# One pool of 2 KB pieces for the second mixer and the expert layer, seven weight chunks made of pieces, and a gather in fp32 from the residual stream

## The chip, the cores and the metric

The kernel runs on one core of a Trainium2 chip. The metric is the device time of one execution in microseconds (us), taken as the median of several runs. Lower is better. The engines are TensorE (PE in the rows, its weight loads PEld), VectorE (DVE), ScalarE (ACT), GpSimd (POOL) and SyncE (SP), which here only issues transfers; 16 DMA engines move data between DRAM and the on-chip memory of 128 partitions.

## What is computed

Two layers of an encoder over 256 tokens of width 1024. Each layer has a token mixer (attention, RWKV-7, pooling and convolution in four groups of columns) and a channel mixer: a dense SwiGLU in the first layer, and eight experts of which each token takes two in the second. The change touches the memory of the second mixer and the whole of the expert layer, which computes this (the reference sorts the tokens by expert; the sum is the same):

```python
h = rms_norm(x, norm_g[l, 2]) * (1.0 + sc_f) + sh_f
logits = xf @ router_w                       # 256 x 8
top_val, top_idx = lax.top_k(logits, 2)
gates = jax.nn.softmax(top_val, axis=-1)
# for every expert e, over the tokens that chose it:
y_e = (jax.nn.silu(xblk @ w1[e]) * (xblk @ w3[e])) @ w2[e]
out = out.at[tok].add(y_e * gate[:, None])
x = x + gt_f * rms_norm(out, norm_g[l, 3])
```

An expert's three matrices are 1024 x 3584, 1024 x 3584 and 3584 x 1024 in fp32, so the eight experts are 336 MB of weights, and every one of them is read once for a few dozen tokens.

## The kernel before

The program is laid out by a recording layer and pools: the code says what reads and writes which tile, a tile pool decides when its memory may be taken again, and the order in which an engine's instructions stand is made from that. The stages follow one another: modulation, mixer 0, dense layer, mixer 1, expert layer. In the profiled execution the last one begins at about 640 us.

**Weights of the experts.** The packed weights of an expert are 42 chunks (`NCH`) of 128 partitions x 2048 fp32, 1 MB each: 28 for the first two matrices and 14 for the third. `weights()` (L970) hands out the next buffer of a ring of 13 and issues its load on SyncE, with no condition but that the buffer's last reader is done. The ring has three kinds: three `raw` buffers and four pairs `hi`, `lo` of half the width, which earlier stages use for their own weights, and six (`MRAW`) of the expert layer's own, `mw`. A `raw` or `mw` chunk is one DMA, with 8 KB per partition in a row (L985); a pair is two DMAs with 4 KB rows (L979). A DMA on SyncE also waits until the one eight places ahead of it has landed, and SyncE issues in one fixed order, so whatever waits there holds back all that stands behind.

**One expert.** `up()` takes the chunks of the first two matrices (products `u`), `gated()` makes silu(u1) x u3 and transposes it (`sg`, `sT`), `down()` takes the chunks of the third (`y`). This goes in four pieces of the hidden width (`SUP`, index `s`), with `down` of one piece behind `up` of the next. The tokens of an expert sit in up to 96 places (`CAP`), in three groups of 32; the third is computed only if there are more than 64 tokens. `outputs()` and `back()` then spread the result over the 256 tokens (`yhl`, `oT`), weight it and add it to `yac`.

**Router and gather.** The router's logits `lg` come from matmuls `pl`; VectorE picks the two best (`MAX`, `MAX_INDEX`), makes `selb`, and TensorE the places of the tokens (`pos`), from which `posm`. The gather is a matmul with a one-hot matrix `oh`. Since a product in the format fp32r (a faster format of less precision) is inexact, the normalised tokens are first split into a high part `hh` and a low part `hl` by `natural()` (L1038 to L1042), and `gather()` (L1056) runs two fp32r matmuls for each block, for two experts at once (2 x 96 columns). It is called by `prepare()` for a pair of experts: at the start, and for the next pair in piece `s == 1` of every second expert.

**The place where the layer starts.** `count()` counts the tokens of each expert (`cnt`), and decides whether any has more than 96 (`of`). `over(0)` reads that flag into a register on several engines, SyncE among them, with a TENSOR_LOAD (L1305), to run a further round if needed; for this input none runs. The load stands in SyncE's order among the DMAs of the weights, where the recording put it. TensorE and others read their own counts.

**Memory.** The mixers use 36 `slots` of [128, 512] fp32 (`NSLOT`) and 38 of [128, 256] (`NHALF`) in a pool of their own that closes at the mixer's end; the expert layer has separate tiles.

## Time and profile before

| what | us |
|---|---|
| median of 3 runs (lowest to highest) | 1511.33 (1510.83 to 1512.97) |
| the profiled execution's own time | 1509.55 |
| its span, first to last instruction | 1507.8 |
| TensorE busy | 1400.7 |
| VectorE busy | 609.9 |
| ScalarE busy | 391.9 |
| GpSimd busy | 1.8 |

The share of TensorE is 93% of the span, and its mean granted clock 0.992 of full speed. The times of the three runs lie within 0.15% of each other. The rows that follow below come from the one profiled execution; microseconds in them count from the start of its span. The page shows the span in 40 equal slices (37.7 us each), with the rate of the transfers in GB/s in each. A table of stretches gives, for every stretch, the busy time of each engine with the number of its instructions, then the granted clock, the share of time in which the 16 DMA engines are busy, and the rate. A timeline lists instructions in order of time, those of one kind in a row together: start, time from the first start to the last end, engine, line, operation, output <- inputs, shapes, count, and in brackets how long the engine idled before and what it waited for. For SyncE it shows the issue of DMAs, not their transfer.

### The profile page before, as it was taken

What the parts mean: (1) busy time and instruction counts of PE and PEld (TensorE: products, weight loads), DVE (VectorE), ACT (ScalarE), POOL (GpSimd) and SP (SyncE); (2) the same over time, 40 slices, a digit from 0 to 9 for tenths busy, and PEclk for the clock granted to TensorE, in tenths of its full rate; (3) what the DMA queues carried; (4) which work ended last, traced back from release to release, by engine and by line L of the source; (5) the groups of instructions that cost most, each with busy time, mean ns of one, the idle gap of its engine ahead of it and who ended that gap; (6) DMA issues with size and microseconds to landing.
All of it is one profiled execution on the core that took longest, in us unless ns stands there. A gap on an engine that the chain in (4) does not pass through costs nothing. (4 is left out here: it accounts for less than half of the span.)

```text
span 1507.8 us, 30915 instructions
## 1 busy us (share of the span) xinstructions
PE 1400.7 (93%) x13541; PEld 824.0 (55%) x13566; DVE 609.9 (40%) x1202; ACT 391.9 (26%) x744; POOL 1.8 (0%) x19
## 2 busy tenths in 40 slices
PE   3999989999998999989898999999999999998885
PEld 2997779999997987733232333333433334332222
DVE  7698879888836785531020020020020200210203
ACT  4744464444438643420020000010000010000101
POOL 0000000000000000000000000000000000000000
PEclk9999999999999999999999999999999999999998
DMA  9554659978733421579999999999999999999994
GB/s 375 207 202 136 205 231 388 367 290 313 291 137 130 158 79 37 216 300 417 418 416 416 416 415 416 416 411 379 416 416 415 416 417 416 416 404 412 416 409 198
DMA packets 85262, 487.43 MB, mean 323 GB/s; under 512 B 9841, under 2 KB 10225, under 8 KB 40946
## 3 DMA queue, kind: packets, MB, share of 16 engines
q1 hardware_dynamic: 83522, 482.45, 80.3%
q10 hardware_dynamic: 1584, 2.68, 0.6%
q8 instruction: 124, 2.03, 0.5%
q14 instruction: 32, 0.26, 0.0%
HBM read 484.05 MB, written 1.05 MB: 322 GB/s over the span
## 5 line engine op out<-in xcount | busy, mean ns | idle before, releaser
L167 PE MATMUL u<-mw,xe 128*32 128x512 f32 (+1 forms) x3368 | 358.6, 537 | 22.2 <-DMA mw<-in_moe_dram 18.0
L1158 DVE TENSOR_TENSOR sg<-sg,u 128x256 f32<-128x256 f32 (+1 forms) x96 | 34.3, 381 | 651.3 <-ACT sg L1157 651.3
L167 PEld LDWEIGHTS u<-mw,xe 128*32 128x32 f32 x3368 | 115.1, 109 | 218.2 <-issue 159.8
L1157 ACT ACTIVATE sg<-u 128x256 f32<-128x256 f32 (+1 forms) x96 | 30.8, 356 | 666.8 <-PE u L167 657.4
L167 PE MATMUL y<-mw,sT 128*32 128x512 f32 x1480 | 180.9, 594 | 18.7 <-DMA mw<-in_moe_dram 13.4
L218 DVE TENSOR_TENSOR wlo<-raw,whi 128x1024 fp32r<-128x1024 f32 x142 | 170.2, 1222 | 51.9 <-ACT whi L217 51.5
L217 ACT ACTIVATE whi<-raw 128x1024 fp32r<-128x1024 f32 x142 | 147.1, 1057 | 146.5 <-issue 50.4
L167 PE MATMUL u<-mwhi,xe 128*32 128x512 f32 (+1 forms) x748 | 172.2, 551 | 1.8 <-DMA mwhi<-in_moe_dram 1.0
L167 PE MATMUL u<-mwlo,xe 128*32 128x512 f32 (+1 forms) x748 | 151.4, 551 | 1.5 <-issue 0.8
L171 PE MATMUL g<-hlo,whi 128*128 128x256 f32 x448 | 127.1, 284 | 0.2
L170 PE MATMUL g<-hhi,whi 128*128 128x256 f32 x448 | 127.1, 284 | 0.0
L172 PE MATMUL g<-hhi,wlo 128*128 128x256 f32 x448 | 126.8, 283 | 0.0
L167 PEld LDWEIGHTS y<-mw,sT 128*32 128x32 f32 x1480 | 53.2, 109 | 129.8 <-issue 84.0
L254 DVE CUSTOM_DVE_ANT_0 raw<-raw,row,pcs 128x1024 f32<-128x1024 f32 x96 | 120.3, 1279 | 4.2 <-ACT row L1341 3.7
L167 PE MATMUL y<-mwhi,sT 128*32 128x512 f32 x324 | 95.8, 594 | 0.0
L170 PE MATMUL z<-hhi,whi 128*128 128x256 f32 x304 | 88.1, 290 | 3.8 <-ACT whi L217 3.7
L167 PEld LDWEIGHTS u<-mwhi,xe 128*32 128x32 f32 x748 | 46.9, 109 | 79.1 <-issue 69.1
L172 PE MATMUL z<-hhi,wlo 128*128 128x256 f32 x304 | 87.2, 287 | 2.4 <-DVE wlo L218 2.4
L171 PE MATMUL z<-hlo,whi 128*128 128x256 f32 x304 | 88.1, 290 | 0.2
L171 PEld LDWEIGHTS g<-hlo,whi 128*128 128x128 f32 x448 | 86.1, 192 | 1.2 <-DVE hlo L336 0.7
L170 PEld LDWEIGHTS g<-hhi,whi 128*128 128x128 f32 x448 | 86.2, 193 | 0.6
L172 PEld LDWEIGHTS g<-hhi,wlo 128*128 128x128 f32 x448 | 86.2, 192 | 0.0
(302 smaller groups left out, 1825.0 us busy)
## 6 DMA issues: line engine op xcount, KB each, us to landing
mw<-in_moe_dram SPq DMA_DIRECT2D x232, 1024.0 KB, 15.1
mwlo<-in_moe_dram SPq DMA_DIRECT2D x104, 512.0 KB, 12.6
mwhi<-in_moe_dram SPq DMA_DIRECT2D x104, 512.0 KB, 13.8
raw<-in_ada_dram SPq DMA_DIRECT2D x44, 1024.0 KB, 6.6
raw<-in_ffn_dram SPq DMA_DIRECT2D x42, 1024.0 KB, 7.0
raw<-in_win_dram SPq DMA_DIRECT2D x20, 1024.0 KB, 4.8
raw<-in_wout_dram SPq DMA_DIRECT2D x6, 1024.0 KB, 4.9
raw<-in_ada_dram SPq DMA_DIRECT2D x8, 512.0 KB, 6.9
```

What stands on the lines that cost most here:

```text
L167: pe.matmul(o, a, b, start=start, stop=stop)
L170: pe.matmul(o, ah, bh, start=start, stop=False)
L171: pe.matmul(o, ah, bl, start=False, stop=False)
L172: pe.matmul(o, al, bh, start=False, stop=stop)
L217: ops[0].append(act.activation(hi, raw[:, c], AF.Copy))
L218: ops[1].append(dve.tensor_sub(lo, raw[:, c], hi.bitcast(F32)))
L254: r = dve.tensor_tensor_reduce(w, w, cB, scale=1.0, scalar=P(l, "ab", v * KB + k), op0=OP.mult, op1=OP.add, accum_out=mods[l][:, v, k:k + 1])
L1157: other_set(act.activation(sg, u[:, 0:w], AF.Silu))
L1158: dve.tensor_mul(sg, sg, u[:, w:2 * w])
```

## The change

- One pool for mixer 1 and the expert layer: 55 slots of [128, 512] fp32, 2 KB per partition. It stays open from mixer 1 to the end; mixer 0 has a pool of the same form that closes. The 38 half-size tiles of the mixers are now halves of slots (`halves`), made in pairs.
- The ring of weight buffers has 17 chunks, in this order: seven of kind `slots`, each of four slots and loaded with four DMAs with 2 KB rows; three `raw`; four pairs; three `mw` (`MRAW` from 6 to 3).
- The expert layer's other large tiles (`hT`, `yac`, `oh`, `xe`, `dg`, `oT`, `sg`, `sT`, `yhl`) are slots too, and `prow` lies in the memory of an earlier constant.
- `natural()`, `hh` and `hl` go. The gather is an fp32 matmul from the residual stream `xr` with `oh` scaled by the norm `rs`, one expert at a time (96 columns), prepared in piece `s == 1` of every expert but the last.
- The loads `lr`, `c` and `pw` of mixer 1, which stood behind three loads of its weights, now stand among the loads of the dense layer.

```diff
-NSLOT = 36
-NHALF = 38
-MRAW = 6
+NSLOT = 55
+MRAW = 3
+MSLOT = 7
...
+    def slots(st, name):
+
+        sp = st.enter_context(tc.tile_pool(name=name, bufs=1, reuse_waits="tile"))
+        return lambda name, dt=F32: sp.tile([128, 512], dt, name=name, tag="s", bufs=NSLOT)
...
-            def half(name):
-                return mp.tile([128, 256], F32, name=name, tag="h", bufs=NHALF).rearrange("p (n f) -> p n f", n=4)
+            def halves(name):
+                t = slot_(name).rearrange("p (e n f) -> p e n f", e=2, n=4)
+                return [t[:, e] for e in range(2)]
...
-            ring = ["raw"] * NR + ["half"] * (2 * NH) + ["m"] * MRAW
+            ring = ["slots"] * MSLOT + ["raw"] * NR + ["half"] * (2 * NH) + ["m"] * MRAW
             mw = {"n": 0}
 
             def weights(src, first=None):
                 kind = ring[mw["n"] % len(ring)]
                 mw["n"] += 1
-                if kind == "half":
-                    hs = [wp.tile([128, 1024], F32, name="mw" + t, tag=t, bufs=2 * NH) for t in ("hi", "lo")]
-                    for i, h in enumerate(hs):
-                        nc.sync.dma_start(h, src[:, i * 1024:(i + 1) * 1024])
-                    return lambda c, n: hs[c // 1024][:, c % 1024:c % 1024 + n]
-                if kind == "raw":
-                    t = wp.tile([128, 2048], F32, name="mw", tag="raw", bufs=NR)
+                if kind == "slots":
+                    ts = [slot_("mws") for _ in range(4)]
+                elif kind == "half":
+                    ts = [wp.tile([128, 1024], F32, name="mw" + t, tag=t, bufs=2 * NH) for t in ("hi", "lo")]
+                elif kind == "raw":
+                    ts = [wp.tile([128, 2048], F32, name="mw", tag="raw", bufs=NR)]
                 else:
-                    t = ep.tile([128, 2048], F32, name="mw", tag="mw", bufs=MRAW)
-                nc.sync.dma_start(t, src)
-                return lambda c, n: t[:, c:c + n]
-
-            hh = one.tile([128, 2, D], F32R, name="hh")
-            hl = one.tile([128, 2, D], F32R, name="hl")
+                    ts = [ep.tile([128, 2048], F32, name="mw", tag="mw", bufs=MRAW)]
+                w = 2048 // len(ts)
+                for i, t in enumerate(ts):
+                    nc.sync.dma_start(t, src[:, i * w:(i + 1) * w])
+                return lambda c, n: ts[c // w][:, c % w:c % w + n]
...
-            yac = one.tile([128, 2, D], F32, name="yac")
-
-            def natural():
-                for tb in range(2):
-                    act.activation(hh[:, tb, :], xr[:, tb, :], AF.Identity, scale=rs[:, tb:tb + 1])
-                    for c in HALF:
-                        dve.scalar_tensor_tensor(hl[:, tb, c], xr[:, tb, c], rs[:, tb:tb + 1],
-                                                 hh[:, tb, c].bitcast(F32), op0=OP.mult, op1=OP.subtract)
...
-            def gather(cols, w):
-
-                xe = ep.tile([128, KB, w], F32, name="xe", tag="xe", bufs=2)
+            def gather(pos):
+
+                oh = slot_("oh").rearrange("p (b s) -> p b s", b=2)[:, :, 0:CAP]
+                for tb in range(2):
+                    dve.tensor_scalar(oh[:, tb, :], C("iota")[:, 0:CAP], pos[:, tb:tb + 1], rs[:, tb:tb + 1],
+                                      op0=OP.is_equal, op1=OP.mult)
+                xe = [v4(slot_("xe"))[:, :, 0:CAP] for _ in range(2)]
 
                 def step(k2):
-                    p = pa("gx").rearrange("p (j t) -> p j t", j=2)
+                    p = pa("gx").rearrange("p (j t) -> p j t", j=2)[:, :, 0:CAP]
                     for j in range(2):
                         ks = slice((2 * k2 + j) * 128, (2 * k2 + j + 1) * 128)
-                        n = 0
-                        for s in (hh, hl):
-                            for tb in range(2):
-                                mm(p[:, j, 0:w], s[:, tb, ks], cols[:, tb, 0:w], n == 0, n == 3)
-                                n += 1
+                        for tb in range(2):
+                            mm(p[:, j, :], xr[:, tb, ks], oh[:, tb, :], tb == 0, tb == 1)
                     for j in range(2):
                         k = 2 * k2 + j
-                        act.activation(xe[:, k, :], p[:, j, 0:w], AF.Identity, scale=gcol[l][:, 2, k:k + 1],
-                                       bias=mods[l][:, SH_F, k:k + 1])
+                        act.activation(xe[k // 4][:, k % 4, :], p[:, j, :], AF.Identity,
+                                       scale=gcol[l][:, 2, k:k + 1], bias=mods[l][:, SH_F, k:k + 1])
 
                 return xe, [lambda k2=k2: step(k2) for k2 in range(KB // 2)]
-
-            def onehot(dst, ps):
-                for tb in range(2):
-                    dve.tensor_scalar(dst[:, tb, :], C("iota")[:, 0:CAP], ps[:, tb:tb + 1], None, op0=OP.is_equal)
...
-            prow = one.tile([128, NE, T], BF, name="prow")
-
-            def prepare(pr):
-
-                oh = ep.tile([128, 2, 2, CAP], F32R, name="oh", tag="oh", bufs=2)
-                for j in range(2):
-                    onehot(oh[:, :, j, :], posm[:, :, 2 * pr + j])
-                if pr == 0:
-                    natural()
-                xe, steps = gather(oh.rearrange("p b j s -> p b (j s)"), 2 * CAP)
-                for j in range(2):
-                    xes[2 * pr + j] = (xe, j * CAP)
+            prow = cB.bitcast(BF).rearrange("p (e t) -> p e t", e=NE)
+
+            def prepare(e):
+                xes[e], steps = gather(posm[:, :, e])
...
-                if e % 2 == 1 and e + 1 < NE:
-                    if s == 1:
-                        return prepare((e + 1) // 2)
+                if s == 1 and e + 1 < NE:
+                    return prepare(e + 1)
...
-    mixer(0, [lambda v=v, ch=ch: ada_chunk(0, v, ch) for v in FV for ch in range(4)])
+    with ExitStack() as st:
+        mixer(0, [lambda v=v, ch=ch: ada_chunk(0, v, ch) for v in FV for ch in range(4)], slots(st, "sl0"))
...
+    slot_ = slots(ctx, "sl1")
+    mixer(1, [lambda: moe_router(1)], slot_)
```

SyncE, where the loads of the experts' weights begin (`mw` a chunk in one DMA, `mwhi` and `mwlo` half of one, `mws` a quarter; `of` is the register load). Before:

```order
L985 DMA mw<-in_moe_dram 128x2048 x3
L979 DMA mwlo<-in_moe_dram 128x1024
L979 DMA mwhi<-in_moe_dram 128x1024 x2
L979 DMA mwlo<-in_moe_dram 128x1024 x2
L979 DMA mwhi<-in_moe_dram 128x1024
L979 DMA mwlo<-in_moe_dram 128x1024
L979 DMA mwhi<-in_moe_dram 128x1024
L985 DMA mw<-in_moe_dram 128x2048 x6
L1305 TENSOR_LOAD of
L1305 ISA x2
```

Now, from the last pair of the four:

```order
L980 DMA mwhi<-in_moe_dram 128x1024
L980 DMA mwlo<-in_moe_dram 128x1024
L980 DMA mw<-in_moe_dram 128x2048 x2
L980 DMA mws<-in_moe_dram 128x512 x4
L1279 TENSOR_LOAD of
L1279 ISA x2
L980 DMA mws<-in_moe_dram 128x512 x15
L1095 UNCONDITIONAL_BRANCH
L980 DMA mws<-in_moe_dram 128x512 x9
L1095 UNCONDITIONAL_BRANCH
L980 DMA mw<-in_moe_dram 128x2048
```

Before, the thirteen chunks of the ring stand in the order in which they are read, all ahead of the register load. Now the ten chunks of the three other kinds, three of them whole ones of `raw` at the head as before, stand ahead of the seven made of `mws`, which are read first; one of the seven is ahead of the register load, six are behind it, and then come refills, the first of them a whole chunk. (The branches are those around the third token group, at which every engine's program is cut.)

VectorE, between the two halves of the router's choice of experts (tokens 0 to 127, then 128 to 255; `m`, `i` are the best values and their places). Before:

```order
L1016 MAX m_7288<-lg 128x8
L1017 MAX_INDEX i_7289<-m_7288,lg 128x8
L1042 SCALAR_TENSOR_TENSOR hl<-xr,rs,hh 128x512 x2
L1014 SCALAR_TENSOR_TENSOR lg<-pl,rs,lb 128x8
L1042 SCALAR_TENSOR_TENSOR hl<-xr,rs,hh 128x512
L1016 MAX m_7288<-lg 128x8
L1042 SCALAR_TENSOR_TENSOR hl<-xr,rs,hh 128x512
L1017 MAX_INDEX i_7289<-m_7288,lg 128x8
L1046 TENSOR_TENSOR gw<-m_7288 128x2
```

Now:

```order
L1008 MAX m_7237<-lg 128x8
L1009 MAX_INDEX i_7238<-m_7237,lg 128x8
L1006 SCALAR_TENSOR_TENSOR lg<-pl,rs,lb 128x8
L1008 MAX m_7237<-lg 128x8
L1009 MAX_INDEX i_7238<-m_7237,lg 128x8
L1031 TENSOR_TENSOR gw<-m_7237 128x2
L1019 TENSOR_TENSOR sel_7308<-cs,i_7238 128x16
```

The four `hl` rows are gone from between the two halves.

The gather's matmuls, which wait for this on TensorE, were sixteen pairs of 128x192 with `hh` and `hl` ahead of `cnt`, and are now sixteen of 128x96 with `xr`.

## Rows read from the trace of the kernel before

**Rows 1.** The page: GB/s moved in 40 equal slices of the span.

```profile
GB/s 375 207 202 136 205 231 388 367 290 313 291 137 130 158 79 37 216 300 417 418 416 416 416 415 416 416 411 379 416 416 415 416 417 416 416 404 412 416 409 198
```

**Rows 2.** Stretches: bounds, us, busy PE PEld DVE ACT POOL, clock, DMA share, GB/s.

```profile
600.00:620.00 20.00, 20.00 (x256) 14.82 (x255) 7.42 (x24) 3.71 (x7) 0.52 (x1) 1.00 0.43 153
620.00:640.00 20.00, 18.10 (x183) 15.12 (x178) 13.45 (x34) 11.97 (x37) 0.00 (x0) 1.00 0.69 253
640.00:660.00 20.00, 16.14 (x114) 8.66 (x113) 11.30 (x49) 8.36 (x15) 0.00 (x0) 0.91 0.59 245
660.00:680.00 20.00, 19.30 (x162) 6.44 (x167) 2.27 (x6) 1.04 (x3) 0.00 (x0) 1.00 0.94 368
680.00:1000.00 320.00, 301.95 (x2759) 107.00 (x2760) 39.68 (x96) 23.82 (x59) 0.00 (x0) 1.00 1.02 416
1000.00:1040.00 40.00, 40.00 (x365) 14.03 (x368) 2.26 (x6) 3.79 (x9) 0.00 (x0) 1.00 0.98 377
1040.00:1480.00 440.00, 414.45 (x3865) 147.98 (x3872) 59.48 (x140) 29.20 (x76) 0.00 (x0) 1.00 1.01 414
```

**Rows 3.** DMA issues: output, queue, count, KB each, median us from issue to landing.

```profile
mw<-in_moe_dram SPq DMA_DIRECT2D x232, 1024.0 KB, 15.1
...
mwlo<-in_moe_dram SPq DMA_DIRECT2D x104, 512.0 KB, 12.6
...
bi<-in_rpb_dram ACTq DMA_DIRECT2D x8, 256.0 KB, 2.6
...
out_dram<-xr SPq DMA_DIRECT2D x2, 256.0 KB, 2.2
```

**Rows 4.** Short stretches with one kind of row in flight, columns as in rows 2.

```profile
691.00:701.00 10.00, 9.17 (x86) 2.37 (x80) 0.00 (x0) 0.00 (x0) 0.00 (x0) 1.00 1.01 421
...
705.00:710.00 5.00, 5.00 (x52) 1.70 (x48) 2.26 (x6) 1.04 (x3) 0.00 (x0) 1.00 1.02 405
...
1503.60:1506.20 2.60, 0.00 (x0) 0.00 (x0) 1.06 (x2) 0.00 (x0) 0.00 (x0) 0.50 1.02 379
...
561.60:563.00 1.40, 1.40 (x44) 1.29 (x38) 1.37 (x5) 0.77 (x3) 0.00 (x0) 1.00 0.69 187
```

**Rows 5.** Timeline of SyncE's queue, 628 to 710 us, issues of DMAs.

```profile
632.89 28.60 SPq L985 DMA_DIRECT2D mw<-in_moe_dram  x9
...
671.90 13.10 SPq L985 DMA_DIRECT2D mw<-in_moe_dram  x9
...
704.58 0.33 SPq L979 DMA_DIRECT2D mwlo<-in_moe_dram  x1
```

**Rows 6.** What SyncE waited for, 440 to 665 us: total, times, longest.

```profile
SPq L1305 <- DVE osec L1234: 16.1, 1, 16.1
...
SPq L985 <- PE u L167: 7.7, 1, 7.7
```

**Rows 7.** Timelines of VectorE and TensorE around the gather, 636 to 664 us.

```profile
639.93 1.41 DVE L1042 SCALAR_TENSOR_TENSOR hl<-xr,rs,hh 128x512 fp32r<-128x512 f32 x2
...
642.13 0.74 DVE L1042 SCALAR_TENSOR_TENSOR hl<-xr,rs,hh 128x512 fp32r<-128x512 f32 x1
...
644.12 0.80 DVE L1078 TENSOR_SCALAR oh<-cs,posm 128x96 fp32r<-128x96 f32 x4
...
651.41 0.16 DVE L1232 TENSOR_SCALAR of<-oc 128x8 int32<-128x8 f32 x1
...
637.11 3.84 PE L167 MATMUL pl<-rtg,hT 128*128 128x128 f32 x32
...
644.89 0.51 PE L167 MATMUL gx<-oh,hh 128*128 128x192 f32 x2 [1.10 <-DVE oh L1078]
...
650.22 0.21 PE L167 MATMUL cnt<-selb,onesb 128*128 128x8 bf16 x2
650.36 1.92 PE L167 MATMUL u<-mw,xe 128*32 128x512 f32 x16
```

**Rows 8.** What TensorE waited for, 640 to 1508 us: total, times, longest.

```profile
PE u L167 <- DMA mw<-in_moe_dram: 18.0, 33, 0.7
```

More of the change, by code (lines that the diff above doesn't have):

```diff
@@ L525, in rw_core @@
                 ark = n8("ark")
-                X, nT, XT, ak, sB, sK, sV, Ub, Sb = [[None, None] for _ in range(9)]
+                X, nT, XT, ak, sV, sB, sK = [halves(n) for n in ("X", "nT", "XT", "ak", "sV", "sB", "sK")]
                 def pq(name):
@@ L541, in rw_core @@
                         mmh(p[:, c], ar[e][:, c, 0], R["B"][:, e, c])
-                    nT[e] = half("nT")
                     dve.tensor_mul(nT[e], p, b4(m3[:, e, None, :]))
-                    XT[e] = half("XT")
                     yield
                 for lv in range(NLV):
-                    P1 = [None, None]
+                    P1 = halves("P1")
                     for e in range(2):
@@ L577, in rw_core @@
                                 mmh(p[:, c], R[nm][:, e, c], C("i2"))
-                            b = half("s" + nm)
-                            act.activation(b, p, AF.Copy)
-                            (sV, sB, sK)[lv - 1][e] = b
+                            act.activation((sV, sB, sK)[lv - 1][e], p, AF.Copy)
                             yield
-                for e in range(2):
-                    Ub[e] = half("Ub")
-                    Sb[e] = half("Sb")
+                Ub, Sb = halves("Ub"), halves("Sb")
                 for i in range(4):
@@ L995, in moe_layer @@
             pls = []
-            hTs = one.tile([128, 2, 2, 4, 128], F32, name="hT", tag="yhl")
             for tb in range(2):
                 pl = pa("pl")[:, 0:128]
-                hT = [hTs[:, tb, 0], hTs[:, tb, 1]]
+                hT = [v4(slot_("hT")) for _ in range(2)]
                 for k4 in range(2):
@@ L1186, in outputs @@
             def outputs(x):
-                x.yhl = one.tile([128, 2, NG, 512], F32R, name="yhl", tag="yhl")
+                x.yhl = [[slot_("yhl", F32R) for _ in range(NG)] for _ in range(2)]
                 for g in range(NG):
-                    act.activation(x.yhl[:, 0, g, :], x.y[g], AF.Copy)
-                    dve.tensor_sub(x.yhl[:, 1, g, :], x.y[g], x.yhl[:, 0, g, :].bitcast(F32))
+                    split(x.yhl[0][g], x.yhl[1][g], x.y[g])
             def back(x, tb, first):
@@ L1334, in moe_layer @@
             use_lnexp()
-            residual([[yac[:, tb, h] for h in HALF] for tb in range(2)], out)
+            residual(yac, out)
     for hf in range(2):
```

47 lines of the change are left out of this document (21 added, 26 removed).

## Prediction

> **What bounds the kernel now.** I read the speed of the transfers slice by slice first, then a table of stretches for the last two thirds, then the rows around the place where the expert layer begins, since the diff touches little else. In the slices [rows 1] the transfers run at 404 to 419 GB/s from about 680 us to the end, with two dips to 379 and 404, and well below that nearly everywhere earlier. The table [rows 2] says the same: from 680 to 1480 us the 16 DMA engines are busy all the time (share 1.01 to 1.02), and TensorE 95% of it. TensorE is the waiting one: in the expert layer its largest wait is for weight chunks, 18.0 us in 33 pieces [rows 8]. So this stage lasts as long as 336 chunks of 1 MB take to move, and what matters is the price of a chunk, and when the stream gets to full speed.
>
> The price depends on the rows that a chunk is cut into. Before, 232 chunks move as one DMA whose rows are 8 KB per partition, 104 as two DMAs of 4 KB rows [rows 3]. In the order of issue [rows 5] there are stretches with only one kind in flight: 8 KB rows in 691 to 701 us (the nine DMAs issued between 672 and 685 us are the ones moving), 4 KB rows in 705 to 710 us. These give 421 and 405 GB/s at a full share [rows 4]; over seven such 4 KB stretches I read 405 to 412 and take 409. A chunk of 1.0486 MB is then 2.49 us in 8 KB rows and 2.56 us in 4 KB rows, and the mix is (232 x 2.49 + 104 x 2.56) / 336 = 2.512 us. Against that, the 800 us from 680 to 1480 move (320 x 416 + 40 x 377 + 440 x 414) / 1000 = 330.4 MB, or 315.1 chunks, which at 2.512 are 791 us: 9 us are lost in that stretch, some 4 of them in 1000 to 1040.
>
> The start is the weak stretch. From 640 to 660 us the share is only 0.59 [rows 2]. SyncE issues nothing there: its nine DMAs that begin at 632.89 stretch to 661 [rows 5], because it first stands 16.1 us at the register load of `of` (L1305), and then 7.7 us for TensorE to give a buffer back [rows 6]. Transfers sum to 3.1, 5.1, 4.9 and 7.4 MB in the four stretches from 600 to 680 us; with half a chunk before 600, that is 19.9 chunks by 680.
>
> **The change part by part.** *Smaller rows.* The built program shows how the 336 chunks now divide: 117 in 8 KB rows, 79 in 4 KB rows, and 140 as four DMAs each of 2 KB rows. The last kind is in no stretch of the expert layer. Three readings bound it. From below: it could cost what 8 KB rows cost, 2.49. Linear in the number of rows, 128 more rows per chunk cost 2.56 - 2.49 = 0.07 (0.075 before rounding), so 512 rows cost 2.49 + 3 x 0.075 = 2.71. The output store at the end of the kernel has 2 KB rows in 256 KB DMAs, at a share of 1.02: 379 GB/s [rows 3, 4], so 2.77. From above: one 256 KB load of `bi`, alone in the queues, reaches 187 GB/s at a share of 0.69, or 271 at a full share, so 3.87; it counts its own beginning and end, which a stream has hidden. I take 2.74, between the two nearest rows: one is the same stream in the same direction, extended by a step, and the other has the same row and DMA size, but writes to DRAM.
>
> All chunks then cost 117 x 2.49 + 79 x 2.56 + 140 x 2.74 = 877.2 us, against 232 x 2.49 + 104 x 2.56 = 843.9 before: +33.3 us. Issuing is no bound: a DMA takes SyncE about 0.4 us, four make 1.6, under 2.74.
>
> The Trainium skill has a rule on this, in "DMA: Bandwidth & Descriptors", section "Why small descriptors are slow (HBM only)": every packet costs about 3 cycles over its 32-byte beats, and packing pays only at 256 bytes or less. An estimate from that page gives 2 KB rows (4 x 67) / 259 of the 8 KB price, 2.58 us, and the sum would be near +6. By the same rule 4 KB rows would be 1.2% dearer than 8 KB rows; the rows show 2.8%, so the trace does not agree, and it has weight only in a rival below.
>
> *Gather.* `natural()` goes: two ScalarE operations of 1024 elements and four VectorE ones (1.41 + 0.74 + 0.74 us), which stand between the two halves of the router's choice on VectorE, and two of the four one-hot operations ahead of the first matmul [rows 7]. Of those 2.9 us on VectorE some 1.3 lie on the path to `selb`, and two one-hots of 0.2 us fewer: the first gather matmul comes at 643.2 instead of 644.89. The old one takes until `cnt` at 650.22. The new has 16 fp32 matmuls of 96 columns; 16 fp32 ones of 128 columns (`pl`) take 3.84 us [rows 7], so `cnt` comes by 647.0 and `of`, 1.2 us after it, at 648.2 instead of 651.4. Later gathers lie inside the stream, where TensorE has 5% of idle time: 7 x 16 matmuls of at most 0.24 us, 27 us, for 3 x 32 of 0.17 us, 16 us. That is 11 us more in 800, under the 40 us that it idles there; a slower stream only widens this cover. I cost it at nothing.
>
> *Start of the stream.* Two things work against each other. The ring has 17 chunks instead of 13, but its first seven (the 2 KB kind) lie in memory that the mixer still uses. In the new order on SyncE eleven chunks go ahead of the register load (7 to 15, 28, and chunk 0), 24 pieces for chunks 1 to 6 stand behind it, and behind those the refill with chunk 20, which waits until TensorE has finished chunk 7. Before, thirteen chunks go ahead of the load, all of the ring. The eleven are there in time: at the pace of before 8.2 chunks had moved by 640 us, and 2.8 more take 7. So: the register load ends at about 648.4; the pieces move from 649.5 to 649.5 + 6 x 2.74 = 666; TensorE gets the last of them at 667, has chunk 7 done at some 669.5 (a chunk in two token groups is 1.92 us [rows 7]) and the refill flows from 670.5. By 680 us that makes 17 + 9.5 / 2.49 = 20.8 chunks, against 19.9: a lead of 0.9 chunks, -2.3 us, uncertain by 5 either way. Until 670 the transfers stand still twice for 4 to 5 us, where before they stood once for longer. After this start the new order leaves at least 6 MB of transfers between a buffer's last reader and its refill, as the old one did, so no further stop.
>
> *From 680 us on.* Of the 877.2 us the first 20.8 chunks hold 7 x 2.74 + 9 x 2.49 + 4.8 x 2.56 = 53.9; 823.3 remain. Before, 843.9 - 19.9 x 2.512 = 793.9 remain. The difference is +29.4, in which the lead is counted. The dip at 1000 to 1040, where TensorE is busy all the time and the transfers wait for it (377 GB/s, 3.8 us lost), should partly vanish when the transfers are slower: -1.4. Sum: **+28 us**. The mixers and the dense layer keep their instructions, with loads of mixer 1 issued somewhat earlier while TensorE is the busy one there; I cost that at nothing, give or take 3. What stands behind the last chunk is unchanged but for buffers.
>
> The profiled execution takes 1509.55 us, the median of the runs is 1511.33. The sum gives 1537.5 for an execution like the profiled one, and 1511.33 + 28 = **1539** as the median.
>
> **The rivals.** *Small rows cost nothing* (faster). If the 2 KB pieces go at 2.49, the 133 of them after 680 us save 133 x 0.25 = 33 us of the sum: 28 - 33 = -5, so 1506. The fact that shares read 1.02 for all kinds of rows is for it; the step of 2.8% from 8 to 4 KB rows and the 379 GB/s of the store are against. The sign turns at a price of 2.74 - 28 / 133 = 2.53. *They cost a little*, 2.53 to 2.65: a time of 1511 to 1527, with the page's estimate at 1517.5 among them. *The stream stops again* (much slower). SyncE issues in one order, and the refills are no longer in the order in which chunks are read: chunks 29 to 31 go ahead of 16 to 19 once. Each such place makes TensorE wait for three chunks, 8 us; if that delays the release of a buffer, for which the next DMA in the order waits, the transfers stand still as well. With 17 chunks of cover this costs nothing as long as TensorE is less than 6 MB (15 us) behind; beyond that it would come back in each expert, and three such stops make 1539 + 24 = 1563. *The change doesn't do what it says*: the pool's order could hold the first pieces until the mixer's last reader, beyond the register load; the start then loses 5 more, 1544.
>
> **How the numbers follow.** The forecast, with a price of 2.65 to 2.80 (+16 to +36 with the start's error of 5): 0.74, own range 1530 to 1549. Small rows for nothing: 0.09. A little: 0.08. Stops, or a price toward the upper bound: 0.09. The range reaches down to 1514, which takes in most of the third, and up to 1556, which takes in the slower start and the mild stops; what is left out is the free price and the repeated stops, some 0.17. A measurement tells 0.2% from no change, that is 3 us: faster means below 1508.3 (0.09), the same up to 1514.4 (0.04), slower above it (0.87).
>
> **What would show it.** In the trace after: windows of the stream near 400 GB/s at a full share, and near 380 where only pieces are in flight; TensorE idle longer for chunks; the end of the transfers some 28 us later. The start: `of` at 648, chunk 20's DMA near 670. If the stream runs at 414 or more with pieces in it, the price is wrong, and with it the sign. If the share falls below 0.9 after 690, the third rival holds.

## The result and the profile after

The changed kernel takes 1579.05 us (median of 4 runs, 1574.65 to 1580.68) against 1511.08 for the kernel before: a ratio of 1.0443, with a 95% interval of 1.042 to 1.0467. It is 68 us slower, where 28 were forecast. Its profiled execution took 1579.75 us, with a span of 1577.8.

The page of the kernel after, GB/s in 40 slices, now 39.4 us wide (to be held against [rows 1]):

```profile
GB/s 377 179 195 135 194 260 381 349 317 325 269 54 151 151 23 91 262 278 381 394 396 389 392 389 402 390 390 388 384 389 391 402 359 394 398 372 386 382 390 209
```

From the slice at about 710 us on the stream runs at 359 to 402 GB/s; before, from about 680 us on, it ran at 379 to 418. Four marks show where the 70 us between the two spans came from. The last row of mixer 1's residual on VectorE, before and after (line, operation, count, shortest, median and longest time in ns, first and last start in us):

```profile
L353 DVE SCALAR_TENSOR_TENSOR xr<-ya,rs,xr x8: 740/743/754, 205.0 to 635.7; 128x512 f32<-128x512 f32 x8
```

```profile
L353 DVE SCALAR_TENSOR_TENSOR xr<-ya,rs,xr x8: 740/740/751, 214.5 to 647.5; 128x512 f32<-128x512 f32 x8
```

The first of the eight starts ends mixer 0: 205.0 to 214.5, 9.5 us later. The last ends mixer 1: 635.7 to 647.5, so 11.8 us are lost before the expert layer begins, in these two executions. Then two stretches of the transfers, each pair with about the same amount moved (columns as in [rows 2]). Before:

```profile
590.00:696.00 106.00, 99.28 (x967) 57.05 (x969) 41.56 (x134) 29.30 (x69) 0.52 (x1) 0.98 0.67 263
696.00:1483.00 787.00, 743.15 (x6855) 264.85 (x6878) 99.16 (x236) 55.76 (x141) 0.00 (x0) 1.00 1.01 413
```

After:

```profile
590.00:717.00 127.00, 119.15 (x1133) 70.93 (x1137) 44.39 (x142) 34.50 (x88) 0.00 (x0) 1.00 0.61 216
717.00:1553.00 836.00, 808.27 (x6998) 326.59 (x7018) 100.37 (x251) 62.36 (x165) 0.00 (x0) 1.00 1.02 389
```

The first 28 MB, counted from 590 us (263 GB/s x 106 us, 216 x 127), are there 21 us later. Of these 11.8 are the mixers'; some 9 are lost at the layer's start. The next 325 MB take 836 us in place of 787: 49 us in the stream. What follows the stream is 24.8 us in both (1507.8 - 1483, 1577.8 - 1553). So 12 + 9 + 49 = 70. The forecast had 0, -2 and +30.

The share of the DMA engines is 1.02 in the slow stream: they are as busy as before and move less. The pieces as they were issued (columns as in [rows 3]):

```profile
mws<-in_moe_dram SPq DMA_DIRECT2D x560, 256.0 KB, 6.0
...
mw<-in_moe_dram SPq DMA_DIRECT2D x117, 1024.0 KB, 11.4
...
mwlo<-in_moe_dram SPq DMA_DIRECT2D x79, 512.0 KB, 10.2
```

A stretch of the kernel after in which only pieces are in flight (columns as in [rows 2]):

```profile
708.00:713.00 5.00, 5.00 (x33) 2.09 (x32) 0.00 (x0) 0.00 (x0) 0.00 (x0) 1.00 1.05 365
```

At 365 GB/s a chunk costs 2.87 us, against 2.74 in the sum. The rate is not steady: over all 23 stretches of more than 4 us in which the packets of the trace are of pieces alone it lies between 330 and 388 GB/s, with a mean of 362 (2.90 us).

The start, on SyncE and TensorE (columns as in [rows 5, 7], then two stretches as in [rows 2], then SyncE's waits from 600 to 720 us as in [rows 6]):

```profile
645.97 32.14 SPq L980 DMA_DIRECT2D mws<-in_moe_dram  x28
689.46 0.33 SPq L980 DMA_DIRECT2D mw<-in_moe_dram  x1
```

```profile
655.04 3.81 PE L167 MATMUL gx<-oh,xr 128*128 128x96 f32 x32 [0.71 <-DVE oh L1045]
658.69 0.19 PE L167 MATMUL cnt<-selb,onesb 128*128 128x8 bf16 x2
661.53 1.92 PE L167 MATMUL u<-mws,xe 128*32 128x512 f32 x12 [2.64 <-DVE dg L1069]
```

```profile
680.00:685.00 5.00, 5.00 (x49) 1.82 (x42) 0.00 (x0) 0.00 (x0) 0.00 (x0) 1.00 0.26 100
685.00:690.00 5.00, 4.82 (x38) 1.81 (x36) 0.54 (x2) 0.92 (x3) 0.00 (x0) 1.00 0.01 3
```

```profile
SPq L980 <- PE u L167: 18.7, 5, 11.3
SPq L1279 <- DVE osec L1217: 11.9, 1, 11.9
```

The gather did as forecast: `cnt` comes 11.2 us after the last residual row (658.69 - 647.5), against 14.5 before and 11.3 in the sum. But the first weight matmul waits another 2.6 us, for VectorE's four `dg` operations, which now stand together in front of it. And after the 28 pieces SyncE stands 11.3 us at the refill, the first whole chunk behind them (689.46 us), which waits for TensorE; the transfers stand still from 682.3 to 690.4 us. That refill comes 42 us after the end of mixer 1; the sum had 34.8.

### The profile page after: what moved, and what is told of

Same layout as the page of the kernel before. It is cut to its first block, busy times and chain, and to the rows that moved or that the text cites. A ratio compares the mean times of both kernels' runs of the same rounds, so it can differ in the third digit from the quotient of the medians.

```text
span 1577.8 us, 31672 instructions
## 1 busy us (share of the span) xinstructions
PE 1482.2 (94%) x13669; PEld 899.6 (57%) x13694; DVE 608.5 (39%) x1206; ACT 397.4 (25%) x774; POOL 1.8 (0%) x19
## 3 DMA queue, kind: packets, MB, share of 16 engines
HBM read 484.05 MB, written 1.05 MB: 307 GB/s over the span
## 5 line engine op out<-in xcount | busy, mean ns | idle before, releaser
L167 PE MATMUL u<-mws,xe 128*32 128x512 f32 (+1 forms) x1992 | 284.9, 540 | 8.0 <-issue 2.8
L167 PE MATMUL u<-mw,xe 128*32 128x512 f32 (+1 forms) x1920 | 234.2, 527 | 8.4 <-DMA mw<-in_moe_dram 4.0
L167 PEld LDWEIGHTS u<-mws,xe 128*32 128x32 f32 x1992 | 102.2, 109 | 135.6 <-issue 97.6
L167 PE MATMUL y<-mws,sT 128*32 128x512 f32 x936 | 159.4, 605 | 8.7 <-DMA mws<-in_moe_dram 4.5
L167 PEld LDWEIGHTS u<-mw,xe 128*32 128x32 f32 x1920 | 81.1, 109 | 106.4 <-issue 83.3
L167 PE MATMUL u<-mwhi,xe 128*32 128x512 f32 (+1 forms) x476 | 121.4, 573 | 0.3 <-PEq L1095 0.2
L167 PE MATMUL u<-mwlo,xe 128*32 128x512 f32 (+1 forms) x476 | 114.0, 572 | 0.6 <-issue 0.3
L167 PEld LDWEIGHTS y<-mws,sT 128*32 128x32 f32 x936 | 50.1, 110 | 95.5 <-issue 62.1
L167 PE MATMUL y<-mw,sT 128*32 128x512 f32 x616 | 97.1, 594 | 2.7 <-DMA mw<-in_moe_dram 1.8
```

What stands on the lines that cost most here:

```text
L167: pe.matmul(o, a, b, start=start, stop=stop)
```

## The experiments

**What a chunk in 2 KB pieces costs.** Seven kernels are the kernel before with only the loads of the six `m` buffers changed, which carry 154 of the 336 chunks. The first cuts them as the change does:

```diff
-                nc.sync.dma_start(t, src)
+                    for i in range(4):
+                        nc.sync.dma_start(t[:, i * 512:(i + 1) * 512], src[:, i * 512:(i + 1) * 512])
```

> The kernel before, in which each chunk of kind m (154 of the 336) is loaded by four DMAs with 2 KB rows into the same buffer; the ring, its order and everything else stay. It measures the price of such a chunk alone. Theory A (a chunk in 2 KB pieces costs some 2.93 us, as the whole stream of the changed kernel at 390 GB/s would have it): 154 x (2.93 - 2.49) = +68 us. Theory B (it costs 2.74, as predicted, and the rest of the loss is the new order of issue and the start): 154 x 0.25 = +39 us. If pieces cost nothing: 0.

Measured: 1571.99 us against 1512.09, ratio 1.0396 (1.0368 to 1.0423), +60 us. The pieces alone, with no new ring, gather or pool, cost nearly what the whole change costs, on 154 chunks in place of 140. Of the two theories that is nearer to A. A stretch of this kernel with six such chunks in a row, then two parts of it:

```profile
714.00:734.00 20.00, 19.85 (x185) 8.60 (x180) 1.47 (x6) 0.72 (x3) 0.00 (x0) 1.00 1.00 356
716.00:724.00 8.00, 7.85 (x82) 3.23 (x79) 0.00 (x0) 0.00 (x0) 0.00 (x0) 1.00 1.04 387
724.00:732.00 8.00, 8.00 (x82) 3.77 (x81) 1.03 (x5) 0.72 (x3) 0.00 (x0) 1.00 0.95 303
```

356 GB/s is 2.95 us for a chunk, but within the stretch lie 387 and 303: the price is not a fixed amount on every piece. The packets of the traces say the same. From 720 to 1440 us half of the 2 KB packets take at most 84 ns, here as in the next kernel, but 2.5% take more than 150 ns here and 0.4% there. Then the number of DMAs and the length of the rows were taken apart:

```diff
+                    t = ep.tile([128, 4, 528], F32, name="mw", tag="mw", bufs=MRAW)
+                    nc.sync.dma_start(t[:, :, 0:512], src.rearrange("p (a f) -> p a f", a=4))
```

> As the run with quarters, but each m chunk is one DMA whose rows are cut into 2 KB by a gap of 64 bytes in the buffer after every 512 elements: as few DMAs as before, but short rows. If the rows make the price, it is as slow as the run with quarters, +39 to +68 us; if the number of DMAs does, it is within 5 us of before.

Measured: 1530.33 us, 1.012 (1.0103 to 1.0137), +18 us. Short rows in one DMA cost little: this stretch of six chunks gives 400 GB/s, 2.62 us.

```profile
712.00:727.00 15.00, 13.09 (x145) 5.44 (x137) 0.00 (x0) 0.00 (x0) 0.00 (x0) 1.00 1.04 400
```

So it was neither end: the rows make 18 of the 60 us, the pieces as DMAs the rest. The counterpart, four DMAs with long rows, was first cut by blocks of partitions:

```diff
+                    for i in range(4):
+                        nc.sync.dma_start(t[i * 32:(i + 1) * 32], src[i * 32:(i + 1) * 32])
```

> As the run with quarters, but the four DMAs of a chunk take 32 partitions each, with rows of 8 KB: as many DMAs, but rows as long as before. If the number of DMAs makes the price (SyncE issues a DMA only when the one eight places ahead has landed, so less is in flight), it is as slow as the run with quarters, +39 to +68 us. If the length of the rows makes it, it is within 5 us of before.

Measured: 1912.12 us, 1.2665 (1.2617 to 1.2714), +400 us. This told nothing on the question, since something else became far worse: the DMA engines are busy all the time and move 281 GB/s. An 8 KB packet takes 561 ns in the median here (720 to 1440 us), where it took 312.

```profile
680.00:1000.00 320.00, 238.72 (x1768) 74.46 (x1760) 28.32 (x70) 18.36 (x45) 0.00 (x0) 0.92 1.00 281
```

With every fourth partition in place of 32 neighbours the same number of rows can be asked fairly (each DMA then reads 8 KB out of every 32 KB of DRAM):

```diff
-                        nc.sync.dma_start(t[i * 32:(i + 1) * 32], src[i * 32:(i + 1) * 32])
+                        nc.sync.dma_start(t[i::4], src[i::4])
```

> As the run with four DMAs of 32 partitions and 8 KB rows, which took 400 us more, but each DMA takes every fourth partition instead of 32 neighbours. If the neighbours are the cause (all DMA engines write into the same quarter of the memory), it falls to within 20 us of before, and tells what four small DMAs with long rows cost. If so few rows for one DMA are the cause, it stays above 1800 us.

Measured: 1553.38 us, 1.0281 (1.0264 to 1.0297), +42 us, more than the 20 expected. The neighbours were the cause of some 360 of the 400; the other 42 are what four DMAs of 256 KB cost with rows as long as before. The remaining steps vary size and place. Two DMAs of 512 KB, 2 KB rows cut by gaps:

```diff
+                    for i in range(2):
+                        nc.sync.dma_start(t[:, 2 * i:2 * i + 2, 0:512],
+                                          src[:, i * 1024:(i + 1) * 1024].rearrange("p (a f) -> p a f", a=2))
```

> As the run in which each m chunk is one DMA cut into 2 KB rows by gaps (18 us slower than before), but as two DMAs of half the columns each. With four DMAs without gaps it was 60 us slower. If each further DMA of a chunk costs the same, one third of the 42 us between them: 1540 to 1548 us. If only DMAs of 256 KB are too small for eight in flight, it is as fast as with one DMA: 1527 to 1534 us. If the gap in the buffer is what made the other run fast, it is near the run with four: 1560 to 1572 us.

Measured: 1532.08 us, 1.0139 (1.0122 to 1.0157), +21 us, as with one DMA. Four DMAs of 256 KB with 2 KB rows, each reading one block of DRAM:

```diff
+                        nc.sync.dma_start(t[:, i * 512:(i + 1) * 512],
+                                          src[32 * i:32 * i + 32].rearrange("a (b f) -> (a b) f", b=4))
```

> As the run with quarters (four DMAs of 256 KB with 2 KB rows, 60 us slower than before), but each of the four reads one block of 256 KB that lies together in DRAM, in place of 2 KB out of every 8 KB. The weights come into the buffers in another order, so the output of the experts is not the reference's; amount of data and work are the same. If the scattered reading is what makes the quarters dearer than two DMAs with 2 KB rows (21 us), it falls to 1530 to 1536 us. If it is the small DMAs as such, it stays at 1566 to 1576 us.

Measured: 1550.11 us, 1.0261 (1.0244 to 1.0277), +38 us, between the two answers. Two DMAs of 512 KB that read scattered 2 KB rows:

```diff
+                        nc.sync.dma_start(t.rearrange("p (a b f) -> p a b f", a=2, b=2)[:, :, i, :],
+                                          src.rearrange("p (a b f) -> p a b f", a=2, b=2)[:, :, i, :])
```

> The kernel before, with each m chunk as two DMAs of 512 KB, one for the first and third, one for the second and fourth 2 KB of every partition: DMAs of 512 KB that read scattered 2 KB rows, without gaps in the buffer. Two DMAs of 512 KB that read 4 KB together in DRAM, cut into 2 KB rows, cost 20 us; four of 256 KB cost 38 us reading one block, and 60 us reading scattered rows. If scattered reading costs its 22 us whatever the size of the DMA, 1549 to 1557 us; if it costs only in small DMAs, 1529 to 1536 us.

Measured: 1540.48 us, 1.0193 (1.0176 to 1.021), +29 us, again between: scattering costs some 8 us at 512 KB and 22 at 256 KB. The same stretch, six chunks of kind m in flight, of the four last kernels in the order of the table below (rows 4, 2, 5 and 3 of it):

```profile
714.00:730.00 16.00, 12.96 (x142) 5.47 (x137) 0.00 (x0) 0.00 (x0) 0.00 (x0) 1.00 0.97 370
```

```profile
714.00:726.00 12.00, 11.16 (x141) 4.90 (x134) 0.00 (x0) 0.00 (x0) 0.00 (x0) 1.00 1.04 399
```

```profile
714.00:730.00 16.00, 15.85 (x170) 7.96 (x166) 1.47 (x6) 0.72 (x3) 0.00 (x0) 1.00 1.02 375
```

```profile
714.00:728.00 14.00, 13.24 (x154) 6.45 (x149) 0.37 (x2) 0.56 (x3) 0.00 (x0) 1.00 1.04 387
```

| an m chunk as | GB/s with only these | us for one | whole kernel, us more |
|---|---|---|---|
| one DMA, 2 KB rows | 400 | 2.62 | 18 |
| two of 512 KB, 2 KB rows in pairs that lie together | 399 | 2.63 | 21 |
| two of 512 KB, 2 KB rows scattered | 387 | 2.71 | 29 |
| four of 256 KB, 8 KB rows, every fourth of DRAM and of the partitions | 370 | 2.83 | 42 |
| four of 256 KB, 2 KB rows, one block each | 375 | 2.80 | 38 |
| four of 256 KB, 2 KB rows scattered (the change) | 356 | 2.95 | 60 |
| one DMA, 8 KB rows (before) [rows 4] | 421 | 2.49 | 0 |

Each rate is read in one stretch. From 2.49 to 2.95, short rows make 0.13, DMAs of 256 KB another 0.18, scattered reading the last 0.15. Why a DMA of 256 KB costs more than one of 512 KB stays open; that eight of them in flight are too few was not tried by itself. (With the quarters SyncE issues a DMA 17 ns, in the median, after the one eight places ahead has landed, so 2 MB are in flight with pieces, where it would be 4 MB with halves.) The whole kernel loses less than 154 times the extra price once that is large (for the scattered quarters 71 by the price and 60 measured, for one DMA with 2 KB rows 20 and 18).

The Trainium skill asks for at least 1 MiB for each DMA ("DMA: Bandwidth & Descriptors", section "Rules for kernel authors"). The runs agree in direction, though here 512 KB with short rows was no dearer than 1 MB. The estimate of 2.58 us in the prediction, worked out from that page's price of a packet, is near the 2.62 of short rows in one DMA (0.09 of the 0.13); it left out the size of the DMA.

**The changed kernel without the pieces:**

```diff
-MSLOT = 7
+MSLOT = 0
```

> The changed kernel without the seven chunks made of pieces (MSLOT = 0): pool, mixers and gather stay, and the ring has the ten chunks of the three other kinds. It tells what the pieces cost in place. By the runs that change one thing, the stream after the layer's start gives back some 48 us, but a ring of ten is three chunks shallower at the start than before, and 8 or 9 us are lost in mixer 0: if depth costs what it gave in the rings of 15 and 18 (2.5 us a chunk at the start, none later), 1511 + 8 + 2 + 8 - 2 = 1525 to 1535 us. If the pool or the gather cost in the stream beside the pieces, above 1545. If a ring of ten is too short for the whole stream, also above 1545, with TensorE waiting for chunks and a DMA share below 0.98.

Measured: 1541.13 us, 1.0204 (1.0183 to 1.0224): 38 us less than the change, between two of the answers, 6 above the range of 1525 to 1535 and 4 under 1545. The stream (three stretches, the first at the start):

```profile
640.00:660.00 20.00, 17.61 (x149) 11.40 (x153) 10.60 (x46) 10.76 (x28) 0.00 (x0) 1.00 0.37 145
700.00:1000.00 300.00, 280.24 (x2557) 97.82 (x2556) 33.01 (x87) 24.11 (x62) 0.00 (x0) 0.99 1.01 408
1000.00:1100.00 100.00, 99.75 (x999) 41.25 (x996) 10.27 (x27) 5.82 (x17) 0.00 (x0) 1.00 0.94 370
```

It is back at 408 GB/s, with one stretch at 370 and a share of 0.94. TensorE is busy for 99.75 of 100 us there: the transfers wait for it, as they did from 1000 to 1040 us before [rows 2], now for longer, with three buffers fewer. The pieces cost the change its stream; that they were needed for the depth is not so, as the last runs show.

**The order of the ring.**

```diff
-            ring = ["slots"] * MSLOT + ["raw"] * NR + ["half"] * (2 * NH) + ["m"] * MRAW
+            ring = ["raw"] * NR + ["half"] * (2 * NH) + ["m"] * MRAW + ["slots"] * MSLOT
```

> The changed kernel with one line changed: in the ring of weight buffers the seven chunks made of pieces come last instead of first, so that chunks are issued in the order in which they are read. In the changed kernel the transfers stand still between 680 and 690 us, since the first refill waits for TensorE to finish the first raw chunk, which it can only read after the seven late chunks. Theory (this order is what the start costs, some 10 to 13 us): 1566 to 1570 us, and no stretch after the layer's start with a DMA share under 0.3. Rival (the chunks made of pieces are late in either order, the stop only moves): 1576 to 1582 us. The price of the pieces stays in both.

Measured: 1579.48 us, 1.0455 (1.0431 to 1.0479), the same as the change, the time of the rival. Three stretches of 20 us from 640 on, of the change and of this run:

```profile
640.00:660.00 20.00, 15.32 (x114) 13.23 (x112) 12.11 (x47) 11.28 (x37) 0.00 (x0) 1.00 0.77 283
660.00:680.00 20.00, 18.22 (x102) 5.70 (x105) 2.96 (x8) 3.45 (x5) 0.00 (x0) 1.00 0.86 290
680.00:700.00 20.00, 19.34 (x155) 8.52 (x151) 2.73 (x8) 3.33 (x10) 0.00 (x0) 1.00 0.51 186
```

```profile
640.00:660.00 20.00, 16.52 (x126) 12.81 (x124) 14.04 (x52) 11.38 (x38) 0.00 (x0) 1.00 0.58 209
660.00:680.00 20.00, 19.81 (x167) 7.57 (x166) 2.73 (x8) 4.88 (x11) 0.00 (x0) 1.00 0.65 246
680.00:700.00 20.00, 19.85 (x119) 7.79 (x117) 0.00 (x0) 2.31 (x7) 0.00 (x0) 1.00 1.02 367
```

SyncE in this run: DMAs issued, then its waits from 600 to 720 us:

```profile
643.28 23.72 SPq L980 DMA_DIRECT2D mw<-in_moe_dram  x5
667.11 0.64 SPq L980 DMA_DIRECT2D mwhi<-in_moe_dram  x1
668.29 23.26 SPq L980 DMA_DIRECT2D mws<-in_moe_dram  x24
```

```profile
SPq L1279 <- DVE osec L1217: 15.3, 1, 15.3
...
SPq L980 <- PE u L167: 7.3, 2, 5.7
```

The stop at 680 to 700 (0.51) is gone, but 640 to 660 falls from 0.77 to 0.58 and 660 to 680 from 0.86 to 0.65: the stop only moves. That does not settle the theory, since the edit did not do what was meant. The chunks are not issued in the order in which they are read: three refills of `raw` (the last three of the five `mw`, at 665.7 us) and one pair go out ahead of the pieces, though TensorE reads the pieces first. Nor is it mixer 1 alone that makes the pieces late here: it ends at 645.9 us, and the first piece goes out at 668.3, after SyncE has stood 15.3 us at the register load and 5.7 us for TensorE. What the start would be with the pieces ahead of both was not tried.

**The pairs in the mixers.**

```diff
-            def half(name):
-                return mp.tile([128, 256], F32, name=name, tag="h", bufs=NHALF).rearrange("p (n f) -> p n f", n=4)
+            def halves(name):
+                t = slot_(name).rearrange("p (e n f) -> p e n f", e=2, n=4)
+                return [t[:, e] for e in range(2)]
```

> The kernel before with one part of the change alone: the mixers' half-size tiles are taken in pairs from a pool of 55 slots, in each mixer's own pool; the expert layer is untouched. In the changed kernel mixer 0 ends 9.5 us later (205.0 to 214.5 us) and mixer 1 another 2.3 us later. Theory (the pairs are the cause: a slot comes back only when both halves are done, and three pairs are taken earlier than they are written): the kernel is 9 to 13 us slower than before, and mixer 0 ends near 214. Rival (the lower granted clock of that execution, or the loads of mixer 1 that moved, are the cause): within 3 us of before.

Measured: 1518.12 us, 1.0045 (1.0029 to 1.0062), +6 us: below the range, above the rival; mixer 0 ended at 212.0 us. Undone for mixer 0 alone, in the changed kernel:

```diff
-    with ExitStack() as st:
-        mixer(0, [lambda v=v, ch=ch: ada_chunk(0, v, ch) for v in FV for ch in range(4)], slots(st, "sl0"))
+    mixer0(0, [lambda v=v, ch=ch: ada_chunk(0, v, ch) for v in FV for ch in range(4)])
```

> The changed kernel with one part undone: mixer 0 has its own 36 slots and 38 half-size tiles again. Mixer 0 ended at 214.5 us in the changed kernel, and at 205.0 to 208.2 us in five kernels whose mixer 0 is the old one. Theory (taking the halves in pairs costs mixer 0 some 8 us, and all later stages only move): 1569 to 1573 us, with mixer 0 ending near 206. Rival (other parts of the change delay mixer 0): 1577 to 1581 us.

Measured: 1572.52 us, 1.0399 (1.0383 to 1.0416), 6.5 us less than the change, as the theory had it. Both give 6 of the 12. In the profiled executions mixer 0 with pairs ended at 208.2, 212.0, 212.8 and 214.5 us, with the old tiles between 205.0 (the kernel before, the earliest of twelve) and 208.2. Three stretches within it, before, after, and in the changed kernel with MSLOT = 0, which has the pairs too and ended mixer 0 at 208.2:

```profile
120.00:140.00 20.00, 18.29 (x388) 15.26 (x384) 18.45 (x46) 9.37 (x27) 0.00 (x0) 0.91 0.34 120
140.00:160.00 20.00, 18.79 (x389) 16.34 (x390) 17.37 (x44) 11.29 (x27) 0.00 (x0) 1.00 0.62 203
160.00:180.00 20.00, 18.41 (x231) 13.42 (x227) 17.04 (x48) 6.77 (x12) 0.00 (x0) 1.00 0.60 209
```

```profile
120.00:140.00 20.00, 17.73 (x374) 14.97 (x372) 17.49 (x45) 6.50 (x20) 0.00 (x0) 0.87 0.38 118
140.00:160.00 20.00, 18.03 (x321) 15.25 (x320) 14.65 (x37) 8.73 (x25) 0.00 (x0) 0.84 0.54 188
160.00:180.00 20.00, 17.10 (x196) 14.07 (x194) 15.44 (x40) 8.77 (x16) 0.00 (x0) 0.78 0.62 212
```

```profile
120.00:140.00 20.00, 17.65 (x397) 14.75 (x392) 18.60 (x47) 9.12 (x29) 0.00 (x0) 1.00 0.36 122
140.00:160.00 20.00, 17.01 (x366) 15.17 (x365) 17.10 (x43) 9.82 (x22) 0.00 (x0) 1.00 0.57 197
160.00:180.00 20.00, 17.86 (x201) 13.87 (x202) 16.09 (x45) 7.62 (x14) 0.00 (x0) 0.83 0.59 215
```

In the change TensorE's granted clock is 0.84 and 0.78 from 140 to 180 us, where it was 1.00: part of that time it ran at the lower of its two levels (1.2 in place of 2.4 GHz). In the 20 us ahead it was busy for 17.7 us (18.3 before); with MSLOT = 0 it was busy for 17.65 there, and the clock stayed at 1.00 for the next 20. The work is the same, the gaps are a little larger. The end of mixer 0 goes with the clock: with the pairs it is 208.2 us where one of the three stretches is low (0.83), and 212.0, 212.8 and 214.5 where two or three are; with the old tiles no execution has a low clock (under 0.9) in more than one, and they end by 208.2. So most of the loss in mixer 0 comes together with the lower clock, and how much there is of it differs between kernels whose mixers are the same (208.2 with MSLOT = 0, 214.5 in the change). What follows from the end of mixer 0 to that of mixer 1 takes 430.7 to 431.0 us in the eleven executions with the old tiles in both mixers and 432.4 with the pairs alone, 1.5 us more. Why the pairs bring the lower clock more often was not tried.

**The gather, and a better use of the memory.** The gather alone, on the kernel before (`natural()`, `hh` and `hl` go, one fp32 gather for each expert):

```diff
+                        for tb in range(2):
+                            mm(p[:, j, :], xr[:, tb, ks], oh[:, tb, :], tb == 0, tb == 1)
...
-                if pr == 0:
-                    natural()
```

> The kernel before with the new gather alone: natural() and its two tiles go, each expert is gathered by 16 fp32 matmuls from the residual stream; ring, buffers and mixers as before. In the changed kernel the count of tokens comes 11.2 us after the last residual row of mixer 1 instead of 14.5. Theory (the gather gives some 3 us at the start, and its extra TensorE time later is covered by the transfers): 1505 to 1511 us. Rival (the fp32 matmuls inside the stream cost): 1513 to 1520 us.

Measured: 1513.4 us, 1.0011 (1.0001 to 1.0021): no gain, and at the edge of the rival's range. The start gains a little: from 640 to 660 us the transfers move 283 GB/s, where they moved 245 [rows 2]. But from 1000 to 1040 us, where TensorE is busy all the time and the transfers wait for it, they move 357 GB/s, where they moved 377. The page shows two low slices there, 374 and 373, where one was low before [rows 1]:

```profile
GB/s 374 207 202 132 200 229 389 366 296 308 290 140 125 161 79 37 216 319 416 416 417 417 415 416 417 412 374 373 416 414 415 415 416 417 417 406 417 414 412 191
```

So the extra TensorE time of the later gathers is not wholly covered here. Two more `m` chunks in the memory that is free then:

```diff
-MRAW = 6
+MRAW = 8
```

> The new gather on the kernel before, and the memory that hh and hl held used for two more whole chunks of kind m: a ring of 15 chunks, all in rows of 8 or 4 KB. If the depth of the ring at the layer's start is worth what the transfers lose there (before, the DMA share is 0.59 between 640 and 660 us), two more chunks in the ring give up to 2 x 2.5 us on top of the gather: 1500 to 1506 us. If the start is bound by TensorE giving buffers back and not by depth, as the gather alone, 1505 to 1511 us.

Measured: 1506.17 us, 0.9972 (0.9961 to 0.9982): on the line between the two answers, and 7 us less than the gather alone. And all that fits:

```diff
-MRAW = 6
+MRAW = 11
```

> The kernel before with the new gather, and all the memory that is then free used for whole chunks: eleven of kind m, a ring of 18, one more than the changed kernel has, all in rows of 8 or 4 KB. With two more chunks (ring of 15) the kernel was 5.0 us faster than before. If each further chunk at the layer's start gives another 2.5 us, three more give 7: 1497 to 1501 us. If the depth is used up once the transfers no longer stop at the start, 1503 to 1507 us. If the further chunks lie in memory that mixer 1 frees late, it is no better than the ring of 15, 1505 to 1509 us.

Measured: 1497.44 us, 0.9906 (0.9892 to 0.992): 14 us faster than before, within the first answer's range, and 82 faster than the change. The ring has 18 chunks, all whole or in halves. The start in the rings of 15 and 18, 20 us from 640 on, and with 18 also the stretch in which TensorE is busy all the time:

```profile
640.00:660.00 20.00, 17.78 (x138) 8.88 (x140) 9.10 (x43) 7.02 (x17) 0.00 (x0) 1.00 0.96 389
```

```profile
640.00:660.00 20.00, 17.92 (x130) 10.29 (x129) 9.09 (x43) 7.29 (x18) 0.00 (x0) 0.91 1.01 423
660.00:680.00 20.00, 19.70 (x142) 7.32 (x145) 2.27 (x6) 2.74 (x8) 0.00 (x0) 1.00 1.01 415
1000.00:1040.00 40.00, 40.00 (x372) 13.10 (x368) 2.82 (x8) 2.18 (x6) 0.00 (x0) 1.00 1.02 419
```

Where the share was 0.59 [rows 2], it is 0.96 with 15 and 1.01 with 18: the transfers no longer stop. With 18 the 40 us from 640 on move 4.5 MB more than before, about 11 us of transfers. The dip at 1000 to 1040 us is gone too (419 for 377), worth 4 us more. (In these three kernels the register load of `of` holds nothing back at the start. The gather alone, which has that too, did not gain from it: SyncE stands 22.1 us there until TensorE gives the first buffer back, where before it stood 16.1 at the load and 7.7 for TensorE [rows 6]. By these runs it was the depth of 13 that bound the start.)

## Why the prediction was wrong

**The sign and the place were right**: the transfers bound the kernel, shorter pieces make each chunk dearer, and this outweighs the deeper ring. The time lies 23 us above the range. By the stretches above the sum's three parts each came out higher: the stream +49 for +30, the start +9 for -2, the mixers +12 for 0. Together that is 42 us, the distance between the two spans' 70 and the forecast's 28. None of the three makes the whole of it.

**The price of a piece** is the largest step that failed: 2.74 us in the sum, 2.87 in the change itself and 2.95 in the kernel that changes only that. I had bounds of 2.49 and 3.87, took the two rows that were nearest in row length, and drew the range round these two. The extrapolation from 8 and 4 KB rows counted rows alone, and for rows alone it was even a little high (2.71 against 2.62). Yet the halves of before are DMAs of 512 KB, and two DMAs of that size cost hardly more than one of 1 MB (2.63 and 2.62); the step to 256 KB lay outside what they could show. The store had that size, at 2.77, and four DMAs of 256 KB that each read one block came to 2.80. What no load of before had was 256 KB in scattered rows of 2 KB, which makes the rest. The row with the right size on the load side was the lone `bi` load, at 3.87, and I put its excess down to its beginning and end. With 2.87 to 2.95, 140 chunks cost 53 to 64 us more than whole ones, where the sum had 35.

**The cover**, -1.4 in the sum for the dips in which the transfers wait for TensorE, is not settled. By 2.87 the pieces after the start (some 133) would have made the stream 51 us longer, by 2.95 61, and it became 49; in the kernel with quarters it is 71 by the price and 60 measured. Either the slower stream hides more of the 9 us that were lost before, or pieces cost less where whole chunks are in flight beside them. No run tells the two apart.

**The start** was -2.3 and came out at +9. The register load came when forecast, and the first stop of the transfers was as long as forecast. The pieces behind it moved more slowly: the last was issued at 678.1 us, 30.6 after the end of mixer 1, about when the sum had it landed. TensorE's first matmuls were held by `dg` and then by the late pieces, and chunk 7, the first one of `raw`, was read through only at 689 us. So the second stop took 8 us in place of 4 to 5. I had let TensorE finish chunk 7 2.5 us after the last piece. How much of the 9 us each of these makes was not taken apart.

**The mixers** were costed at nothing, give or take 3, because the instructions stay. They stay, but the two mixers took 12 us more in the profiled execution, about 6 of them shown by single parts; the execution before was the earliest of twelve and that after the latest of four.

**The later gathers** were costed at nothing as well. In the kernel with the gather alone they are not quite free; in the change the slower stream leaves TensorE more room, and no run shows a price there.

**The rivals.** The small price (0.09 and 0.08) did not come true in the change; a price toward the upper bound with a stop (0.09) did. That chance and the range were too narrow for a term with a factor of 140 whose upper bound lay 1.1 us above the value taken. One reading was off without effect: the slices of before [rows 1] go up to 418 GB/s, not 419.

## What to carry to other kernels

Where a stream is bound by the DMA engines, price the DMA by its size as well as its rows: here 512 KB and more, reading what lies together, was the cheap form. A deeper ring is worth something only where the transfers stop, here the first 40 us of the layer and the dip at 1000 us; the seven late buffers of the change brought nothing there, its start took 9 us longer. Before cutting buffers into pieces, count what memory is left for whole ones. Tiles taken in pairs are not the same program, even if every instruction stays (6 us here). And when an edit is meant to change an order, read in the trace whether it did, before the time is read as an answer.

## What was not expected of the hardware

DMAs over 32 neighbouring partitions, with 8 KB rows, brought the stream from 416 to 281 GB/s; over every fourth partition it ran at 392 (both from 680 to 1000 us). DMAs of 512 KB with 2 KB rows move 399 GB/s, those of 256 KB with the same rows 375, with the engines busy all the time in both. And a share of 1.00 to 1.05 does not say that the transfers are at their best: it stood there at 356 as at 421 GB/s. The small DMAs were slow in bursts: in 16 us of one stream the rate was 387 GB/s for one half and 303 for the other, and 2.5% of its 2 KB packets took more than 150 ns, with a median of 84.
